# Sliding-window attention of a hybrid decoder layer: head pairs of one kv head, and a shared tile for both key blocks

## The chip, the cores and the metric

The kernel runs on one core of a Trainium2 chip. Five engines run their own instruction streams side by side and wait for each other through semaphores: TensorE (PE in the profile, its weight loads PEld), VectorE (DVE), ScalarE (ACT), GpSimd (POOL) and SyncE (SP), which here only issues DMAs. The metric is the device time of one execution in microseconds.

## The reference

One decoder layer of 1024 tokens and 1024 channels in float32; 16 learned meta tokens stand ahead of the sequence.

```python
z = rmsnorm(h, g_pre_mix) @ w_in              # q | k | v | x_rec | y_rec
# attention: 8 heads of 64, 2 kv heads (4 heads each), window of 128, one sink a head
valid = (diff >= 0) & (diff < WINDOW) & (kpos >= PAD)
s = where(valid, q k^T * 64**-0.5, NEG)
m = max(max(s), sink);  p = exp(s - m)
o = (p / (sum(p) + exp(sink - m))) @ v
# beside it: causal conv(4) -> gated linear recurrence on x_rec, times gelu(y_rec)
h = h + rmsnorm(concat(o, rec) @ w_out)
h = h + rmsnorm(relu(rmsnorm(h) @ w_ff1)**2 @ w_ff2)
```

Queries and keys are cut into blocks of 128. A query block sees its own key block (the triangle on and below the diagonal) and the one before it (the triangle above the diagonal); the two triangles together hold exactly 128 keys for each query. The block before the first holds only the 16 meta tokens.

## The kernel before

The matrix products are done in a fast float32 format of fewer bits. Operands are split into a high and a low part (`split`, L95 on ACT for the high and L98 on DVE for the low part; `split_scaled`, L116 and L117, the same out of an accumulator with a factor), and `mm3` adds three products (L124, L125, L126: high·high, high·low, low·high).

Stages: x and the meta tokens are loaded, normalised (L209, L215) and transposed. For each of four pieces of rows, `project` computes k, v, the first q and the first x. `put_k` (L355 to L357) takes K out of the accumulator: each kv head's 64 channels are written as high part on their own half of the partitions (ACT, L355), copied to the other half (DVE, L356), and the low part is written on the own half (DVE, L357). The other half of the low tile was set to zero.

Attention goes over four head pairs j and two halves of the sequence. A pair consists of head j and head j + 4, one of each kv head. `scores(j, half, q)` gives, for each head and four query blocks, matmuls of 256 keys (L518, L522), the minimum with mask and sink (L538, DVE), the exponential with its sum (L82, ACT), the reciprocal (L549) and the product with it (L551, DVE, one for each block). `attend(j, half, sn)` comes later: for each head it transposes 8 squares of 128 x 128 (L566, PE), splits them (L95, L98), and multiplies with V in pieces of 128, 256, 256, 256 and 128 queries, high and low each (L577). L591 (ACT) and L592 (DVE) add the two parts of the result. Between `scores` and `attend` of a pair stand other matmuls, taken from a list of fills: the projections q1, x1, q2, x2, x3, q3, y0 to y3. `conv` (L601, L606, DVE) follows each x.

After the attention, `gates(c)` multiplies x by block-diagonal gate weights (348 columns each). Their raw form is a tile of a slot of the kind "e", cleared by POOL (L675) and filled by four DMAs (L679). A sigmoid (L82) follows, then decay, recurrence (L720, L721), output projection and the feed-forward part.

All working tiles are taken from pools of a few kinds ("raw" 2 slots, "ws" 4, "a" 16, "b" 17, "c" 8, "d" 4, "e" 2); a new tile waits until the last user of its slot is done. PSUM has four kinds of two banks each (acc, s, pt, o). A scheduler orders each engine's instructions from priorities; `lut` keeps a written order on ACT's table functions.

Of the kernel before, what the change touches and what calls it, by code (L numbers as in the profile page):

```python
# [16 lines left out]
P = 128  # L17
# [20 lines left out]
def hybrid_layer(  # L38
# [23 lines left out]
    def pair(tag, shape):  # L62
        return slot(tag, shape, F32R), slot(tag, shape, F32R)
# [5 lines left out]
    def f32(ap):  # L69
        return ap.bitcast(F32)  # L70
# [118 lines left out]
        return hi, lo_  # L189

    def w_q(j):
        return load_cols(
            [((w_in, Q_COL + HD * j), HD), ((w_in, Q_COL + HD * (j + 4)), HD)]
        )

    def w_x_chunk(c):
        return load_cols([((w_in, X_COL + P * c), P)])
# [50 lines left out]
    khh = [slot("b", [P, T], F32R) for _ in range(2)]  # L248
    kl = [slot("b", [P, T], F32R) for _ in range(2)]
    HALF = (slice(0, HD), slice(HD, P))  # L250
    for h in range(2):
        nc.gpsimd.memset(f32(kl[h][HALF[1 - h]]), 0.0)

    zero = slot("ws", [P, 512])
    nc.vector.memset(zero, 0.0)
    km = const.tile([P, 4, P], F32R, name="km")
    vm = const.tile([P, 2, P], F32R, name="vm")
    nc.vector.tensor_copy(km.rearrange("p a b -> p (a b)"), zero)
    nc.vector.tensor_copy(vm.rearrange("p a b -> p (a b)"), zero[:, :256])

    flip = [0]

# [59 lines left out]
    xn = normed(0)  # L322
    rk = fetch([(K_COL, P)])
    rv = fetch([(V_COL, P)])
    rq = fetch([(Q_COL, HD), (Q_COL + 4 * HD, HD)], "e")
    load_x(2)
    load_x(3)
    rx = fetch([(X_COL, P)], "e")
# [22 lines left out]

    def put_k(hh, lo, src):
        for h in range(2):
            r, o = HALF[h], HALF[1 - h]
            nc.scalar.copy(hh[h][r], src[r])  # L355
            nc.vector.tensor_copy(hh[h][o], src[r])  # L356
            nc.vector.tensor_tensor(lo[h][r], src[r], f32(hh[h][r]), op=ALU.subtract)  # L357

    def sink_k(acc, t0, n):
        o = 0  # L360
        if t0 == 0:
            m = slice(0, NMETA)
            put_k(
                [km[:, 0, m], km[:, 1, m]], [km[:, 2, m], km[:, 3, m]], acc[:, m]
            )
# [6 lines left out]
    def sink_v(acc, t0, n):  # L372
        nc.scalar.copy(vt[:, t0 : t0 + n], acc)

    def new_q():
# [71 lines left out]
    nc.gpsimd.memset(mask1[:, 0:P], NEG)  # L447
    nc.gpsimd.memset(mask1[:, 0:NMETA], 0.0)
    nc.gpsimd.affine_select(
        out=mask1[:, 0:NMETA], in_=mask1[:, 0:NMETA], pattern=[[1, NMETA]],  # L450
        compare_op=ALU.is_gt, fill=NEG, base=P - NMETA, channel_multiplier=-1,
    )
    nc.gpsimd.tensor_copy(mask1[:, P:256], mask[:, P:256])


    lam = prm[:, :, 7]
# [26 lines left out]
            split(hi, lo, src[..., HALF[h]])  # L483

    pv = bank("o")
    nc.tensor.transpose(pv[:NMETA, :P], vt[:, :NMETA], ident)
    put_v([vm[:NMETA, 0, :], vm[:NMETA, 1, :]], pv[:NMETA, :P])
    for b in range(2):
        pv = bank("pt", (P, 4, P))
        for i in range(4):  # L490
# [10 lines left out]


    def scores(j, half, q):
        sn = [slot("c", [P, 4, 257]) for _ in range(2)]
        negm = small.tile([P, 2, 4], F32, name="negm", tag="negm")
        den = small.tile([P, 2, 4], F32, name="den", tag="den")
        rden = small.tile([P, 2, 4], F32, name="rden", tag="rden")
        for h in range(2):
            nc.vector.tensor_copy(
                sn[h][:, :, 256], nsink[:, j + 4 * h : j + 4 * h + 1].to_broadcast([P, 4])  # L510
            )
        for bp in range(2):
            for h in range(2):
                sp_ = bank("s", (P, 2, 256))

# [11 lines left out]
                for i in range(2):  # L527
                    b = 4 * half + 2 * bp + i
                    if b == 0:
                        qk(sp_[:, i, 0:P], b, km[:, h, :], km[:, 2 + h, :])  # L530
                        qk(sp_[:, i, P:256], b, khh[h][:, 0:P], kl[h][:, 0:P])
                    else:
                        c = slice((b - 1) * P, (b + 1) * P)
                        qk(sp_[:, i, :], b, khh[h][:, c], kl[h][:, c])
                for i in range(2):
                    b = 4 * half + 2 * bp + i
                    k = 2 * bp + i
                    nc.vector.tensor_tensor_reduce(  # L538
                        out=sn[h][:, k, 0:256], in0=sp_[:, i, :],
                        in1=mask1 if b == 0 else mask, scale=-1.0,  # L540
                        scalar=nsink[:, j + 4 * h : j + 4 * h + 1],
                        op0=ALU.add, op1=ALU.min, accum_out=negm[:, h, k : k + 1],
                    )
                    lut(
                        sn[h][:, k, :], sn[h][:, k, :], AF.Exp, scale=-1.0,
                        bias=negm[:, h, k : k + 1], accum_out=den[:, h, k : k + 1],
                    )
        for h in range(2):
            nc.vector.reciprocal(rden[:, h, :], den[:, h, :])  # L549
            for k in range(4):  # L550
                nc.vector.tensor_scalar(  # L551
                    sn[h][:, k, 0:256], sn[h][:, k, 0:256], rden[:, h, k : k + 1],
                    None, op0=ALU.mult,
                )
        return sn

    def attend(j, half, sn):
        flat = [t_.rearrange("p a b -> p (a b)") for t_ in sn]
        for h in range(2):
            ph, pl = pair("c", [P, 1024])  # L560
            for bp in range(2):
                pt = bank("pt")
                for i in range(2):
                    for s in range(2):
                        o = (2 * i + s) * P
                        nc.tensor.transpose(  # L566
                            pt[:, o : o + P],
                            sn[h][:, 2 * bp + i, s * P : (s + 1) * P], ident,
                        )
                c = slice(512 * bp, 512 * bp + 512)  # L570
                split(ph[:, c], pl[:, c], pt)
            po = bank("o")

            def av(kb, oc, n, pc, first, last):
                v = vm[:, h, :] if kb == 0 else vk[h][:, kb - 1, :]
                for k, p_ in enumerate((ph, pl)):
                    nc.tensor.matmul(  # L577
                        po[:, oc : oc + n], v, p_[:, pc : pc + n],
                        start=first and k == 0, stop=last and k == 1,
                        skip_group_check=True,  # L580
                    )

            kb0 = 4 * half
            av(kb0, 0, P, 0, True, False)
            for i in range(3):
                av(kb0 + 1 + i, i * P, 256, P + 256 * i, False, False)
            av(kb0 + 4, 3 * P, P, 7 * P, False, True)

            r, o = HALF[h], HALF[1 - h]
            part, whole = flat[h][r, 0:512], flat[0][r, 512:1024]  # L590
            nc.scalar.copy(part, po[o, :])  # L591
            nc.vector.tensor_tensor(whole, po[r, :], part, op=ALU.add)  # L592
# [139 lines left out]

    def load_wo(kc, tag):
        raw = slot(tag, [P, D])
        if kc < 4:
            nc.sync.dma_start(raw[0:HD, :], w_out[HD * kc : HD * kc + HD, :])
            o = HD * (kc + 4)
            nc.sync.dma_start(raw[HD:P, :], w_out[o : o + HD, :])
        else:
            nc.sync.dma_start(raw, w_out[P * kc : P * kc + P, :])  # L740
        wo_raw[kc] = raw

    wo = [None] * KC
# [600 lines left out]
```

## Time and profile before

| | |
|---|---|
| runs | 982.86, 986.53, 989.44 us (median 986.53) |
| profiled execution | span 984.1 us; no time is given for it apart from the span |
| PE | 955.5 us busy, 97%, 4782 matmuls |
| PEld | 803.2 us, 82% |
| DVE | 680.7 us, 69%, 1002 instructions |
| ACT | 502.3 us, 51%, 809 |
| POOL | 71.9 us, 7%, 108 |
| longest chain | PE 87%, DVE 5%, DMA 4%, ACT 2% |

The span runs from the first to the last recorded instruction. Busy time of PE counts modelled ends of pipelined matmuls, so neighbouring matmuls overlap. The chain is followed back from the last instruction, at each step to what released it. In the rows of groups, `out<-in` names the tiles, `x` the count, then busy time and mean nanoseconds of one, then the idle time ahead of it and who ended it. In the rows of the timeline the first number is the start, the second the length.

### The profile page before, as it was taken

What the parts mean: (1) busy time and instruction counts of PE and PEld (TensorE: products, weight loads), DVE (VectorE), ACT (ScalarE), POOL (GpSimd) and SP (SyncE); (2) the same over time, 40 slices, a digit from 0 to 9 for tenths busy, and PEclk for the clock granted to TensorE, in tenths of its full rate; (3) what the DMA queues carried; (4) which work ended last, traced back from release to release, by engine and by line L of the source; (5) the groups of instructions that cost most, each with busy time, mean ns of one, the idle gap of its engine ahead of it and who ended that gap; (6) DMA issues with size and microseconds to landing.
All of it is one profiled execution on the core that took longest, in us unless ns stands there. A gap on an engine that the chain in (4) does not pass through costs nothing.

```text
span 984.1 us, 12519 instructions
## 1 busy us (share of the span) xinstructions
PE 955.5 (97%) x4782; PEld 803.2 (82%) x4782; DVE 680.7 (69%) x1002; ACT 502.3 (51%) x809; POOL 71.9 (7%) x108
## 2 busy tenths in 40 slices
PE   6799999999999999999999999999999999999995
PEld 6798999889878887888888888888888788888874
DVE  6469997775885687665655465468567776779876
ACT  7356665457944554343555556654433343435331
POOL 4010000000002100000000000000111000002012
PEclk9799999999999999999999999999999999999998
DMA  8002100112134466576522364324678766647762
GB/s 282 23 12 63 25 23 22 43 44 65 65 129 147 149 216 193 173 256 200 197 96 86 97 202 130 106 88 122 167 182 190 182 224 190 193 152 191 226 182 85
DMA packets 89371, 133.28 MB, mean 135 GB/s; under 512 B 13752, under 2 KB 52680, under 8 KB 89312
## 3 DMA queue, kind: packets, MB, share of 16 engines
q1 hardware_dynamic: 81488, 112.04, 35.9%
q0 software_dynamic: 6960, 18.35, 8.8%
q10 hardware_dynamic: 864, 2.10, 0.6%
q8 instruction: 37, 0.61, 0.3%
q14 instruction: 22, 0.18, 0.1%
HBM read 113.60 MB, written 18.87 MB: 135 GB/s over the span
## 4 chain that ended last, share of the span: by engine, by line
PE 87%; DVE 5%; DMA 4%; ACT 2%; issue 1%; POOL 1%; POOLq 0%; SPq 0%; DVEq 0%; ACTq 0%
PE ps_acc L125 10%; PE ps_acc L124 10%; PE ps_acc L126 10%; PE ps_s L126 6%; PE ps_s L124 6%; PE ps_s L125 6%; PE ps_pt L124 6%; PE ps_pt L126 6%; PE ps_pt L125 6%; PE ps_o L125 5%; PE ps_o L124 5%; PE ps_o L126 5%; DMA raw<-in_w_ff_dram 2%; PE ps_o L577 2%; PE ps_pt L566 1%
## 5 line engine op out<-in xcount | busy, mean ns | idle before, releaser
L95 ACT CAST ws<-raw 128x1024 fp32r<-128x1024 f32 (+1 forms) x70 | 71.7, 1025 | 124.9 <-PE ps_o L125 47.7
L98 DVE TENSOR_TENSOR ws<-raw,ws 128x1024 fp32r<-128x1024 f32 (+1 forms) x71 | 84.7, 1194 | 54.7 <-ACT ws L95 54.5
L124 PE MATMUL ps_acc<-a,ws 128*128 128x256 f32 (+2 forms) x256 | 85.8, 335 | 0.1
L125 PE MATMUL ps_acc<-a,ws 128*128 128x256 f32 (+2 forms) x256 | 85.3, 333 | 0.0
L126 PE MATMUL ps_acc<-a,ws 128*128 128x256 f32 (+2 forms) x256 | 84.9, 332 | 0.0
L98 DVE TENSOR_TENSOR b<-b,b 128x1024 fp32r<-128x1024 f32 (+2 forms) x48 | 57.6, 1201 | 26.1 <-PE ps_o L125 18.6
L95 ACT CAST ws<-e 128x1024 fp32r<-128x1024 f32 x42 | 43.8, 1043 | 57.6 <-PE ps_o L125 27.6
L95 ACT CAST b<-b 128x1024 fp32r<-128x1024 f32 (+2 forms) x48 | 49.4, 1030 | 43.5 <-DVE b L860 41.5
L98 DVE TENSOR_TENSOR ws<-e,ws 128x1024 fp32r<-128x1024 f32 x42 | 51.4, 1223 | 21.4 <-ACT ws L95 21.4
L126 PEld LDWEIGHTS ps_acc<-a,ws 128*128 128x128 f32 x256 | 48.2, 188 | 4.4
L124 PEld LDWEIGHTS ps_acc<-a,ws 128*128 128x128 f32 x256 | 48.3, 189 | 4.2 <-ACT c L391 0.3
L125 PEld LDWEIGHTS ps_acc<-a,ws 128*128 128x128 f32 x256 | 48.2, 188 | 3.7
L125 PE MATMUL ps_acc<-ws,b 128*128 128x512 f32 (+1 forms) x120 | 46.5, 388 | 1.1 <-DVE ws L98 1.1
L124 PE MATMUL ps_acc<-ws,b 128*128 128x512 f32 (+1 forms) x120 | 46.3, 386 | 0.9 <-ACT ws L95 0.9
L169 POOL TENSOR_TENSOR rs<-ms,half_pow 128x1 f32<-128x1 f32 (+1 forms) x31 | 21.7, 704 | 347.3 <-DVE ms L165 345.9
L126 PE MATMUL ps_acc<-ws,b 128*128 128x512 f32 (+1 forms) x120 | 46.2, 385 | 0.0
L124 PE MATMUL ps_pt<-ws,b 128*128 128x512 f32 x112 | 44.2, 395 | 0.0
L126 PE MATMUL ps_pt<-ws,b 128*128 128x512 f32 x112 | 44.1, 394 | 0.0
L125 PE MATMUL ps_pt<-ws,b 128*128 128x512 f32 x112 | 44.1, 394 | 0.0
L124 PE MATMUL ps_s<-ws,b 128*128 128x512 f32 x110 | 43.4, 394 | 0.0
L125 PE MATMUL ps_s<-ws,b 128*128 128x512 f32 x110 | 43.3, 394 | 0.0
L126 PE MATMUL ps_s<-ws,b 128*128 128x512 f32 x110 | 43.2, 393 | 0.0
(382 smaller groups left out, 2688.6 us busy)
## 6 DMA issues: line engine op xcount, KB each, us to landing
raw<-in_w_ff_dram SPq DMA_DIRECT2D x66, 512.0 KB, 3.9
e<-in_w_ff_dram SPq DMA_DIRECT2D x47, 512.0 KB, 3.7
d<-in_w_ff_dram SPq DMA_DIRECT2D x12, 512.0 KB, 3.9
s_dram<-d POOLq DMA_DIRECT2D x12, 512.0 KB, 3.8
raw<-in_w_in_dram SPq DMA_DIRECT2D x9, 512.0 KB, 3.9
raw<-in_w_ff_dram POOLq DMA_DIRECT2D x9, 512.0 KB, 7.2
c<-in_x_dram SPq DMA_DIRECT2D x8, 512.0 KB, 8.1
d<-in_x_dram SPq DMA_DIRECT2D x8, 512.0 KB, 5.0
```

Source lines behind the costliest of these rows:

```text
L95: nc.scalar.copy(hi, src)
L98: low = nc.vector.tensor_tensor(lo, src, f32(hi), op=ALU.subtract).ins
L124: nc.tensor.matmul(dst, lh, rh, start=start, stop=False, skip_group_check=True)
L125: nc.tensor.matmul(dst, lh, rl, start=False, stop=False, skip_group_check=True)
L126: last_mm[0] = nc.tensor.matmul(dst, ll, rh, start=False, stop=stop, skip_group_check=True).ins.name
L169: last_pow[0] = nc.gpsimd.tensor_tensor(rs[:n], ms[:n], half_pow[:n], op=ALU.pow).ins.name
L566: nc.tensor.transpose(pt[:, o : o + P], sn[h][:, 2 * bp + i, s * P : (s + 1) * P], ident,)
L577: nc.tensor.matmul(po[:, oc : oc + n], v, p_[:, pc : pc + n], start=first and k == 0, stop=last and k == 1, skip_group_check=True,)
```

## The change

- Head pairs are now heads 2j and 2j + 1, both of kv head g = j // 2. The q weights come by one DMA of 128 columns instead of two of 64, the output weights too.
- K's high and low part are both mirrored to the other half of the partitions by SBUF-to-SBUF DMAs on SP's queue, after the second and the fourth piece; the copies on DVE and the zeros are gone.
- The meta tokens take the last 16 of 128 positions of the block before the first, and the rest of that block is zero, so that all blocks have one shape.
- Scores are handled in pairs of query blocks. POOL adds the exponentials of both key blocks into one 128 x 128 square for each head and block; DVE multiplies all four by the reciprocals at once. Four squares instead of eight are transposed, and split.
- GpSimd cuts each part (high, low) into the two triangles by `affine_select`.
- AV is one matmul of 512 (both heads, both blocks, both triangles where they share keys) and two of 256, high and low each.
- The result tile o_ of `attend` takes a slot of kind "e", and is written in pieces of 64 x 256.

```diff
     def put_k(hh, lo, src):
...
             nc.scalar.copy(hh[h][r], src[r])
-            nc.vector.tensor_copy(hh[h][o], src[r])
...
+    def mirror_k(c):
+        for h in range(2):
+            r, o = HALF[h], HALF[1 - h]
+            for t_ in (khh[h], kl[h]):
+                nc.sync.dma_start(f32(t_[o, c]), f32(t_[r, c]))
...
+        if b == 1:
+            for h in range(2):
+                r, o = HALF[h], HALF[1 - h]
+                nc.sync.dma_start(f32(km[o, h]), f32(km[r, h]))
+            mirror_k(slice(0, 512))
+        elif b == 3:
+            mirror_k(slice(512, T))
...
-        for h in range(2):
-            nc.vector.reciprocal(rden[:, h, :], den[:, h, :])
-            for k in range(4):
-                nc.vector.tensor_scalar(
-                    sn[h][:, k, 0:256], sn[h][:, k, 0:256], rden[:, h, k : k + 1],
-                    None, op0=ALU.mult,
-                )
+            nc.vector.reciprocal(rden, den)
+            one = sn[:, :, 0:P]
+            nc.gpsimd.tensor_tensor(one, one, sn[:, :, P:256], op=ALU.add)
+            nc.vector.tensor_tensor(one, one, rden.to_broadcast([P, 4, P]), op=ALU.mult)
+            pairs.append(sn)
...
+    def attend(j, half, pairs):
+        g = j // 2
+        o_ = slot("e", [P, 512])
+        for bp, sn in enumerate(pairs):
+            mh, ml = pair("c", [P, 4, 2, P])
+            pt = bank("pt", (P, 4, P))
             for k in range(4):
+                nc.tensor.transpose(pt[:, k, :], sn[:, k, 0:P], ident)
+            split(mh[:, :, 1, :], ml[:, :, 1, :], pt)
+            for m in (mh, ml):
+                for side, op, sign in ((0, ALU.is_gt, 1), (1, ALU.is_ge, -1)):
+                    nc.gpsimd.affine_select(
+                        out=m[:, :, side, :], in_=f32(m)[:, :, 1, :],
+                        pattern=[[0, 4], [-sign, P]], compare_op=op, fill=0.0,
+                        base=0, channel_multiplier=sign,
+                    )
+            po = bank("o", (P, 2, 256))
+            mhv, mlv = (m.rearrange("p (h i) s q -> p h (i s q)", h=2) for m in (mh, ml))
...
+            b = 4 * half + 2 * bp
+            av(vk[g][:, b, :], 0, 256, P, True, False)
+            av(vm[:, g, :] if b == 0 else vk[g][:, b - 1, :], 0, P, 0, False, False)
+            av(vk[g][:, b + 1, :], P, P, 3 * P, False, True)
+            c = slice(256 * bp, 256 * bp + 256)
+            for h in range(2):
+                r, o = HALF[h], HALF[1 - h]
+                nc.scalar.copy(o_[r, c], po[o, h, :])
+                nc.vector.tensor_tensor(o_[r, c], po[r, h, :], o_[r, c], op=ALU.add)
         ah, al = at[half][j // 2]
-        split(ah[:, j % 2, :], al[:, j % 2, :], flat[0][:, 512:1024])
+        split(ah[:, j % 2, :], al[:, j % 2, :], o_)
```

More of the change, by code (lines that the diff above doesn't have):

```diff
@@ L250, in hybrid_layer @@
     HALF = (slice(0, HD), slice(HD, P))
-    for h in range(2):
[L252 to L256, printed above, removed]
+    km = const.tile([P, 2, 2, P], F32R, name="km")
     vm = const.tile([P, 2, P], F32R, name="vm")
-    nc.vector.tensor_copy(km.rearrange("p a b -> p (a b)"), zero)
-    nc.vector.tensor_copy(vm.rearrange("p a b -> p (a b)"), zero[:, :256])
+    vmt = const.tile([P, P], F32, name="vmt")
+    nc.gpsimd.memset(f32(km), 0.0)
+    nc.gpsimd.memset(vmt, 0.0)
+    META = slice(P - NMETA, P)
     flip = [0]
@@ L446, in hybrid_layer @@
     mask1 = const.tile([P, 256], F32, name="mask1")
[L447 to L453, printed above, removed]
+    nc.gpsimd.memset(mask1[:, 0 : P - NMETA], NEG)
+    nc.gpsimd.tensor_copy(mask1[:, P - NMETA :], mask[:, P - NMETA :])
     lam = prm[:, :, 7]
@@ L485, in hybrid_layer @@
     pv = bank("o")
[L486 to L487 removed]
+    nc.tensor.transpose(pv[:, :P], vmt, ident)
+    put_v([vm[:, 0, :], vm[:, 1, :]], pv[:, :P])
     for b in range(2):
@@ L503, in scores @@
     def scores(j, half, q):
[L504 to L511, printed above, removed]
-        for bp in range(2):
+        g, pairs = j // 2, []
+        for bp in range(2):
+            sn = slot("c", [P, 4, 257])
+            negm = small.tile([P, 4], F32, name="negm", tag="negm")
+            den = small.tile([P, 4], F32, name="den", tag="den")
+            rden = small.tile([P, 4], F32, name="rden", tag="rden")
+            for h in range(2):
+                nc.vector.tensor_copy(
+                    sn[:, 2 * h : 2 * h + 2, 256],
+                    nsink[:, 2 * j + h : 2 * j + h + 1].to_broadcast([P, 2]),
+                )
             for h in range(2):
@@ L555, in scores @@
[L555 to L576, printed above, removed]
+                        scalar=nsink[:, 2 * j + h : 2 * j + h + 1],
@@ L581, in av @@
                     )
[L583 to L592, printed above, removed]
+            b = 4 * half + 2 * bp
[3 more added lines that the diff above has]
+            c = slice(256 * bp, 256 * bp + 256)
+            for h in range(2):
+                r, o = HALF[h], HALF[1 - h]
+                nc.scalar.copy(o_[r, c], po[o, h, :])
+                nc.vector.tensor_tensor(o_[r, c], po[r, h, :], o_[r, c], op=ALU.add)
         ah, al = at[half][j // 2]
-        split(ah[:, j % 2, :], al[:, j % 2, :], flat[0][:, 512:1024])
+        split(ah[:, j % 2, :], al[:, j % 2, :], o_)
     xc = [None] * NLRU
@@ L734, in load_wo @@
         raw = slot(tag, [P, D])
[L735 to L740, printed above, removed]
+        nc.sync.dma_start(raw, w_out[P * kc : P * kc + P, :])
         wo_raw[kc] = raw
```

38 lines of the change are left out of this document (20 added, 18 removed).

## The prediction

> **What bounds the kernel now.** I read the page's engine shares first, then windows of 50 us, since both programs issue the same TensorE instructions in the same order from the 1593rd of the changed one on (near 290 us); then the groups by form and the timelines.
>
> ```profile
> PE 955.5 (97%) x4782; PEld 803.2 (82%) x4782; DVE 680.7 (69%) x1002; ACT 502.3 (51%) x809; POOL 71.9 (7%) x108
> ...
> raw<-in_w_in_dram SPq DMA_DIRECT2D x9, 512.0 KB, 3.9
> ```
>
> ```profile
> 50.00:100.00 50.00, 49.88 (x379) 47.31 (x378) 40.28 (x122) 29.30 (x80) 2.71 (x4) 1.00 0.15 38
> 100.00:150.00 50.00, 50.00 (x386) 47.94 (x385) 46.95 (x142) 34.52 (x98) 0.00 (x0) 1.00 0.09 22
> 150.00:200.00 50.00, 49.50 (x316) 44.42 (x315) 37.60 (x76) 23.33 (x53) 0.00 (x0) 1.00 0.11 32
> ```
>
> The columns of a window are start and end, its length, busy time of PE, PEld, DVE, ACT and POOL, the granted clock, the DMA share and GB/s. In the stage of the attention PE is busy 149.4 of 150 us at full clock. A matmul taken away there comes off the time as long as nothing else makes PE wait. DVE stands second (46.95 of 50 in the densest window), DMA is at a tenth, and POOL does nothing at all from 100 us on. So the stage is bound by the number and spacing of PE's instructions, and the change moves work to the one engine that is empty.
>
> **PE's part.** A busy time overlaps with that of the next matmul, so the price is the distance of the starts.
>
> ```profile
> 107.63 0.63 PE L577 MATMUL ps_o<-c,b 128*128 128x128 f32 x4
> 108.09 0.38 PE L566 MATMUL ps_pt<-ident,c 128*128 128x128 f32 x2
> 108.23 0.77 PE L577 MATMUL ps_o<-c,b 128*128 128x256 f32 x5
> 108.84 0.84 PE L566 MATMUL ps_pt<-ident,c 128*128 128x128 f32 x6
> 109.44 0.36 PE L124 MATMUL ps_acc<-a,ws 128*128 128x256 f32 x1
> ```
>
> Four 128-wide AV matmuls take 108.09 − 107.63 = 0.46, 0.115 each; five 256-wide ones 0.61, 0.122 each; two and six transposes take 0.14 and 0.60, together 0.093 each. The 128-wide matmul costs nearly what the 256-wide one does. For the new 512-wide form I take the projections at the end of the stage:
>
> ```profile
> 203.03 0.40 PE L124 MATMUL ps_acc<-a,ws 128*128 128x512 f32 x1
> ...
> 208.32 0.40 PE L126 MATMUL ps_acc<-a,ws 128*128 128x512 f32 x1
> ```
>
> These are 23 steps in 5.29 us, 0.230 each. How many there are:
>
> ```profile
> L98 DVE TENSOR_TENSOR c<-ps_pt,c 128x512 fp32r<-128x512 f32 x32 | 21.7, 686 | 5.2 <-PE ps_o L577 2.8 <-ACT c L95 2.2
> ...
> L566 PE MATMUL ps_pt<-ident,c 128*128 128x128 f32 x128 | 19.3, 274 | 0.0
> L577 PE MATMUL ps_o<-c,b 128*128 128x256 f32 x96 | 18.4, 297 | 0.0
> ...
> L551 DVE TENSOR_SCALAR c<-c,rden 128x256 f32<-128x256 f32 x64 | 18.1, 350 | 0.3
> ...
> L592 DVE TENSOR_TENSOR c<-ps_o,c 64x512 f32<-64x512 f32 x16 | 10.9, 684 | 4.1 <-ACT c L591 3.9
> ...
> L577 PE MATMUL ps_o<-c,b 128*128 128x128 f32 x48 | 9.1, 247 | 0.5 <-DVE c L98 0.4
> ...
> L577 PE MATMUL ps_o<-c,vm 128*128 128x128 f32 x16 | 3.4, 232 | 0.0
> ```
>
> Half of the 128 transposes go: 64 × 0.10 (between 0.093 here and 0.115) = 6.4. The AV was 64 × 0.115 + 96 × 0.122 = 19.1; it becomes, per pair of query blocks and pair of heads (16 of them), two 512-wide and four 256-wide matmuls, 16 × (2 × 0.230 + 4 × 0.122) = 15.2. That is 3.9. Together 10.3; with the transposes at 0.115, 11.3. I take 10.7. (If the 512-wide AV, whose source is two pieces of 256, came at 0.25, that would be 32 × 0.02 = 0.6 less.) The score matmuls stay as many, as do the projections.
>
> The Trainium skill speaks against half of this: "TensorE: Matmul & The Clock Gate", section "Wait — 56ns, not 53.3ns?", gives 55.6 ns from start to start at N = 128 and 215.7 at N = 512, so that narrow matmuls cost by their width; by it the AV would save next to nothing and the transposes 64 × 0.0556 = 3.6, as an estimate −3.7 in place of −10.7. The rows above show 0.115 at full granted clock for the 128-wide, and I keep to the rows.
>
> **The start.** With K's high part mirrored by DMA, DVE loses its copies ahead of the low parts.
>
> ```profile
> 28.18 0.42 DVE L356 CAST b<-ps_acc 64x256 fp32r<-64x256 f32 x1
> ...
> 29.70 0.42 DVE L356 CAST b<-ps_acc 64x256 fp32r<-64x256 f32 x1
> 30.14 0.43 DVE L357 TENSOR_TENSOR b<-ps_acc,b 64x256 fp32r<-64x256 f32 x1
> ```
>
> ```profile
> 30.62 5.81 PE L237 MATMUL ps_acc<-a,ws 128*128 128x272 f32 x24 [5.56 <-DVE b L357]
> ```
>
> PE stands 5.56 us until the second low part is written at 30.57. The two copies of 0.42 ahead of it are gone, and two more of a few columns: −1.2 at most, −0.8 at least. I take −1.1. The ten mirror DMAs on SP's queue wait for K's sinks; behind those sinks PE still has its q and x projections of the same piece, 48 matmuls of 256, about 5.6 us at 0.117, and a DMA of a whole weight piece lands in 3.9 us (the row of the page above). I cost them at nothing; without that cover they cost 4 once. The weight pieces queued behind them on SP are for projections a whole head pair later.
>
> **The gates.** The output tile of an attend now takes a slot of the kind ("e", two of them) that holds the raw gate weights. Before, that slot was free at 52 us:
>
> ```profile
> 51.99 0.95 POOL L675 MEMSET e<- 128x1024 f32 x1
> 52.97 1.38 SPq L679 DMA_DIRECT2D e<-in_w_a_dram  x2
> ...
> 210.95 0.57 PE L124 MATMUL ps_s<-b,e 128*128 128x348 f32 x2
> 217.45 1.06 ACT L95 CAST b<-d 128x1040 fp32r<-128x1040 f32 x1
> ...
> 219.63 1.28 ACT L82 ACT_TABLE_LOAD   x1
> ```
>
> After, the clearing on POOL, four DMAs and the cast come behind the last attends: 0.95 + 1.4 of issue, 2 to land (half of the 3.9 of a piece of 512 KB) and 1.06 of a cast, about 5.4 us. The second half of y2 (24 × 0.230 = 5.5) just covers it. But the gates then stand without the last attends between them; ACT still has its casts (1.06 each) and the table load (1.28) before the first sigmoid, while PE has only six banks to fill. I reckon 1.28 + 1.06, about 2.4, as lost; at least 0, and at most 5 more if y2 does not cover the weights.
>
> **POOL's part** is the one that decides. For each of 16 block pairs it gets one addition of 128 × 512 and four triangle selections of 128 × 512. Rows near them:
>
> ```profile
> L1237 POOL TENSOR_TENSOR a<-a,a 128x512 f32<-128x512 f32 x3 | 4.0, 1334 | 12.7 <-ACT a L1183 12.7
> ```
>
> ```profile
> 3.44 0.30 POOL L437 MEMSET mask<- 128x256 f32 x1
> ...
> 4.37 0.29 POOL L438 TENSOR_SCALAR_AFFINE_SELECT mask<-mask 128x128 f32<-128x128 f32 x1
> 4.62 0.29 POOL L442 TENSOR_SCALAR_AFFINE_SELECT mask<-mask 128x128 f32<-128x128 f32 x1
> ```
>
> The addition is 1.33. The selection of 512 isn't in the trace; call its price p. If the memset's slope holds, (0.95 − 0.30) / 768 = 0.00085 per element, p = 0.29 + 384 × 0.00085 = 0.62; if everything scales, p = 4 × 0.29 = 1.16; by the distance of the two starts, 4 × 0.25 = 1.0. I take 0.75: memset and selection share their fixed part, 0.085 (0.30 − 256 × 0.00085); of the selection's 0.25 from start to start 0.165 then scale, times four 0.66, and with the fixed part 0.75. In all POOL gets 16 × (1.33 + 4 × 0.75) = 69 us, over the 150 us of the three windows: half, but not evenly. In the changed program's order, laid on the times of before, two stretches are dense: about 104 to 126 with 20 selections and 3 additions, and 137 to 154 with 16 and 2, where each AV stands on PE hardly behind its selections.
>
> The lock. POOL and DVE hold each other up:
>
> ```profile
> 27.40 0.75 DVE L215 TENSOR_SCALAR d<-c,rs 128x1024 f32<-128x1024 f32 x1
> ...
> 52.07 1.41 DVE L215 TENSOR_SCALAR d<-c,rs 128x1024 f32<-128x1024 f32 x1
> ```
>
> ```profile
> 968.51 1.07 DVE L165 SCALAR_TENSOR_TENSOR ms<-sq,late 128x1 f32<-128x1 f32 x1
> ...
> 970.11 0.14 DVE L165 SCALAR_TENSOR_TENSOR ms<-sq,late 128x1 f32<-128x1 f32 x1
> ```
>
> ```profile
> 968.28 1.29 POOL L1237 TENSOR_TENSOR a<-a,a 128x512 f32<-128x512 f32 x1 [12.70 <-ACT a L1183]
> ```
>
> The same operation on DVE takes 1.41 instead of 0.75 beside the memset at 51.99, and a step of 0.14 takes 1.07 until POOL's addition from 968.28 ends. So I count the DVE operations that read two tiles in the on-chip memory as POOL's time in the dense stretches. If all of DVE's work counted (the one at 52.07 reads a single tile), S below would be 0.94 × 39 + POOL's 33.7 − 39, about 31 us, but nothing shows that for the minima and products that make up most of it, so I stay with the two-input ones.
>
> The Trainium skill has a rule for it ("SBUF — State Buffer", "Who interferes with whom"): an exclusive lock of the shared ports, taken when DVE has two such inputs, or works in a two-port mode, and GpSimd reads there. By it the rows just quoted are waits for that lock, and the sum is mine below; the trace of before shows no selection beside a long two-input operation.
>
> ```profile
> 117.39 1.30 DVE L606 SCALAR_TENSOR_TENSOR d<-d,prm,d 128x1039 f32<-128x1039 f32 x1
> ```
>
> ```profile
> L98 DVE TENSOR_TENSOR ws<-raw,ws 128x1024 fp32r<-128x1024 f32 x14 | 17.1, 1223 | 10.1 <-ACT ws L95 10.1
> ...
> L98 DVE TENSOR_TENSOR b<-c,b 128x512 fp32r<-128x512 f32 x8 | 5.4, 686 | 0.7 <-ACT b L95 0.7
> ```
>
> First stretch: three such convolution steps of 1.30 and a first one of 0.8, a weight's low part 1.22, an output's 0.69, and three of the new products of 128 × 512 at 0.69: 8.7. POOL itself 20p + 4.0, in 22 us: 20p − 9.3 too much. Second stretch: 0.8 + 1.22 + 0.69 + 2 × 0.69 = 4.1, POOL 16p + 2.7, in 17 us: 16p − 10.2 too much. Both: S = 36p − 19.5, as PE has nothing else in its order that it could do first: 2.8 at p = 0.62, 7.5 at 0.75, 16.5 at 1.0, 22 at 1.16. What is late next is the score tiles behind it, so that it is not given back. The first two pairs and the last four have 2 to 4 us of other matmuls between selection and AV, and I cost them at nothing.
>
> **DVE and ACT** get lighter: for each of the eight pairs and halves DVE loses eight products (8 × 0.35), two low parts and two additions of 0.69 and gets two products of 0.69 and four additions of some 0.42: 5.6 less 3.1, about −2. They are not what PE waits for, so this counts for nothing but room for the lock.
>
> **Sum**, against the profiled execution's span of 984.1: −10.7 − 1.1 + 2.4 + 7.5 = −1.9, 982.2. The median of the runs shown lies 2.4 above the span: 984.6.
>
> **Rivals.** (1) POOL is hidden: p near 0.62 or the stretches less dense than I lay them, and the gates covered as before. For it: half of POOL's time is free even at 0.75. Against it: the memset and the lock rows. −10.7 − 1.1 = −11.8, 974.7 with the 2.4 between span and median.
>
> (2) Slower: POOL becomes the bound in the dense stretches, because the selection costs by its elements. One mechanism: AV waits for the second pair of selections. It turns the sum at 36p − 19.5 = 9.4, p = 0.80, and passes 1% at p = 1.08. For it: the only two rows of a selection stand at 0.25 to 0.29 for a quarter of the size; a selection beside a DVE operation can only be longer. Against it: the memset's slope. At p = 1.1, S = 20.1, +10.7, 997.2.
>
> (3) The gate weights come late, since POOL's clearing stands behind the last selections: up to 5 more than my 2.4. For it: y2's half covers by 0.5 only. Against it: POOL has 2 to 4 us to spare there. +3.1, 989.6.
>
> **How the numbers follow.** The forecast 0.50, with its own range of 979 (p = 0.62, and the gates' 2.4 partly hidden) to 991 (p = 0.92); rival 1 0.18, rival 2 0.24, rival 3 0.08. The range reaches to rival 1 at 975 and to p = 1.16 of rival 2, +12.6, about 1000. About 1% is what a measurement of this kernel can tell from no change: below 976.7 lies most of rival 1, 0.17; above 996.4 the upper part of rival 2 and what several stalls make together, 0.25; between them 0.58.
>
> **What would show it.** The mean of a selection on POOL (p) and the waits of AV on POOL; PE's idle time from 100 to 155 us, near 7 if I am right, none under rival 1, over 15 under rival 2. DVE's new products longer than 0.69 show the lock. PE's busy time down by some 10, 64 transposes at the old spacing, 512-wide AV at 0.230. The idle time before 36 us shorter by 1. An idle stretch of some 2 us at the gates, ended by ACT; ended by a DMA it is rival 3. Wrong altogether: PE waits for ACT or DVE in the attention, which I cost at nothing.

## The result, and the profile after

The changed kernel takes 981.11 us (median; 979.36 to 983.39), the kernel before 986.22 in the same comparison: a ratio of 0.9941, 95% interval 0.9917 to 0.9965. It is faster, by 0.6%, and inside the 1% that was called no change. The profiled execution's span is 979.4 us against 984.1, 4.7 less where 1.9 less was forecast.

The page's engine shares of the changed kernel, and its windows over the attention (the columns as in the prediction):

```profile
PE 946.1 (97%) x4654; PEld 790.9 (81%) x4654; DVE 666.8 (68%) x957; ACT 496.1 (51%) x810; POOL 142.5 (15%) x186
```

```profile
50.00:100.00 50.00, 49.03 (x365) 46.25 (x364) 38.75 (x117) 28.10 (x80) 17.52 (x18) 1.00 0.16 43
100.00:150.00 50.00, 47.12 (x336) 43.79 (x336) 44.74 (x124) 33.79 (x95) 31.65 (x36) 1.00 0.08 22
150.00:200.00 50.00, 47.91 (x283) 41.86 (x282) 35.96 (x77) 21.68 (x59) 18.15 (x21) 1.00 0.14 43
```

POOL's work went from nothing to 32 of 50 us in the dense window and DVE's fell by 2.2. PE's idle time in the three windows went from 0.1, 0 and 0.5 us to 1.0, 2.9 and 2.1. The groups by form that answer to the rows shown of before:

```profile
L576 POOL TENSOR_SCALAR_AFFINE_SELECT c<-c 128x512 fp32r<-128x512 f32 x64 | 49.7, 796 | 23.2 <-ACT c L95 8.8 <-DVE c L98 7.8 <-DMA raw<-in_w_in_dram 5.5
...
L560 POOL TENSOR_TENSOR c<-c 128x512 f32<-128x512 f32 x16 | 22.8, 1424 | 52.3 <-ACT c L82 52.2
...
L561 DVE TENSOR_TENSOR c<-c,rden 128x512 f32<-128x512 f32 x16 | 13.8, 861 | 5.3 <-POOL c L560 5.1
...
L586 PE MATMUL ps_o<-c,b 128*128 128x512 f32 x32 | 12.2, 402 | 1.6 <-POOL c L576 1.6
...
L572 PE MATMUL ps_pt<-ident,c 128*128 128x128 f32 x64 | 9.8, 273 | 0.0
...
L586 PE MATMUL ps_o<-c,b 128*128 128x256 f32 x56 | 9.2, 280 | 0.0
```

A selection takes 0.80 in the mean, but that is a mixture: 49 of the 64 take 0.63 to 0.67 and 15 take 0.99 to 1.64. The new product on DVE takes 0.86 instead of 0.69. PE's waits from 90 to 165 us, grouped (us in total, times, the longest):

```profile
PE ps_acc L124 <- ACT d L394: 2.2, 3, 0.9
PE ps_o L586 <- POOL c L576: 1.6, 2, 1.2
PE ps_s L526 <- ACT b L116: 1.5, 1, 1.5
PE ps_s L526 <- DVE rden L556: 0.5, 1, 0.5
```

That is 5.9 us of idle time, and only 1.6 of it names POOL directly. The rest names ACT and DVE, which were late in turn. The last two stalls show how, in PE's timeline, then POOL's, DVE's and ACT's. (A row of the timeline names the first form alone: the x6 are two matmuls of 512 columns and four of 256.)

```profile
156.37 1.08 PE L586 MATMUL ps_o<-c,b 128*128 128x512 f32 x6
158.67 1.17 PE L586 MATMUL ps_o<-c,b 128*128 128x512 f32 x6 [1.22 <-POOL c L576]
160.71 0.39 PE L124 MATMUL ps_acc<-a,ws 128*128 128x256 f32 x1 [0.87 <-ACT d L394]
```

```profile
150.76 7.81 POOL L576 TENSOR_SCALAR_AFFINE_SELECT c<-c 128x512 fp32r<-128x512 f32 x7
```

```profile
150.41 1.46 DVE L98 TENSOR_TENSOR ws<-raw,ws 128x1024 fp32r<-128x1024 f32 x1
151.80 1.13 DVE L609 TENSOR_SCALAR d<-d,prm 128x1040 f32<-128x1040 f32 x1
...
153.18 1.33 DVE L614 SCALAR_TENSOR_TENSOR d<-d,prm,d 128x1039 f32<-128x1039 f32 x1
...
155.59 0.82 DVE L517 COPY c<-nsink 128x2 f32<-128x2 f32 x4
...
156.79 1.28 DVE L614 SCALAR_TENSOR_TENSOR d<-d,prm,d 128x1038 f32<-128x1038 f32 x1
...
158.56 1.30 DVE L614 SCALAR_TENSOR_TENSOR d<-d,prm,d 128x1037 f32<-128x1037 f32 x1
```

```profile
159.88 0.37 ACT L599 COPY e<-ps_o 64x256 f32<-64x256 f32 x1 [2.02 <-PE ps_o L586]
160.27 0.66 ACT L394 COPY d<-ps_acc 128x272 f32<-128x272 f32 x2
```

Seven selections take 7.81 us, 1.12 each in the mean. Three of them take 0.63 to 0.67; the other four take 1.09 to 1.61 and lie beside a weight's low part (L98, itself 1.46 where its group in the prediction's rows had 1.22), the convolution's first step (L609, 1.13 where it took 0.80 at 116.39) and its taps (L614). AV waits for the selections. The last tap ends at 159.86, and before that ACT may not copy the next x out of PSUM (L394), since that x takes the slot which the convolution has read. In ACT's queue that copy also stands behind the copy of AV's result (L599), which became free within the same 0.02 us, so this place does not tell which of the two held it. PE has both banks full by then. Another place shows POOL and DVE holding each other up on both sides: an addition that takes 1.29 alone and a selection that takes 0.63, both drawn out around a tap that takes 1.30.

```profile
116.60 1.75 POOL L560 TENSOR_TENSOR c<-c 128x512 f32<-128x512 f32 x1
118.30 1.63 POOL L576 TENSOR_SCALAR_AFFINE_SELECT c<-c 128x512 fp32r<-128x512 f32 x1
```

```profile
117.77 1.68 DVE L614 SCALAR_TENSOR_TENSOR d<-d,prm,d 128x1039 f32<-128x1039 f32 x1
```

The same matmuls, laid side by side from the first to the last, show where the 4.7 us arose: −1.0 at 31 us, −2.2 at 39, −2.4 before the attention, −3.8 at 250 us, behind the attention and the gates, −3.0 at 320 us, −4.5 at the end. The last 1.5 lie in the feed-forward part, which is the same in both programs (the kernel before had two stalls there, 0.37 and 0.88, that the other didn't have); I do not count them as the change's.

### The profile page after: what moved, and what is told of

Its sections match the earlier page's. It is cut to its first block, busy times and chain, and to the rows that moved or that the text cites. A ratio compares the mean times of both kernels' runs of the same rounds, so it can differ in the third digit from the quotient of the medians.

```text
span 979.4 us, 12356 instructions
## 1 busy us (share of the span) xinstructions
PE 946.1 (97%) x4654; PEld 790.9 (81%) x4654; DVE 666.8 (68%) x957; ACT 496.1 (51%) x810; POOL 142.5 (15%) x186
## 4 chain that ended last, share of the span: by engine, by line
PE 78%; DVE 7%; ACT 6%; issue 3%; DMA 3%; POOL 3%; POOLq 0%; DVEq 0%; SPq 0%; ACTq 0%
PE ps_acc L125 8%; PE ps_acc L124 8%; PE ps_acc L126 8%; PE ps_pt L125 6%; PE ps_pt L126 6%; PE ps_pt L124 6%; PE ps_s L126 6%; PE ps_s L125 6%; PE ps_s L124 6%; PE ps_o L124 5%; PE ps_o L125 5%; PE ps_o L126 5%; ACT c L82 2%; DMA d<-in_w_ff_dram 1%; POOL c L576 1%
## 5 line engine op out<-in xcount | busy, mean ns | idle before, releaser
L98 DVE TENSOR_TENSOR ws<-raw,ws 128x1024 fp32r<-128x1024 f32 (+1 forms) x71 | 85.5, 1204 | 51.3 <-ACT ws L95 49.6
L98 DVE TENSOR_TENSOR b<-b,b 128x1024 fp32r<-128x1024 f32 (+2 forms) x48 | 57.6, 1200 | 26.3 <-PE ps_o L125 20.1
L98 DVE TENSOR_TENSOR ws<-e,ws 128x1024 fp32r<-128x1024 f32 x42 | 51.4, 1223 | 20.9 <-ACT ws L95 20.9
L576 POOL TENSOR_SCALAR_AFFINE_SELECT c<-c 128x512 fp32r<-128x512 f32 x64 | 49.7, 796 | 23.2 <-ACT c L95 8.8
L1124 POOL DMA_DIRECT2D raw<-in_w_ff_dram x9 | 10.9, 1208 | 266.1 <-DVE ws L98 200.2
L124 PE MATMUL ps_s<-ws,b 128*128 128x512 f32 x110 | 43.4, 395 | 0.0
```

The source lines that it names most:

```text
L98: low = nc.vector.tensor_tensor(lo, src, f32(hi), op=ALU.subtract).ins
L124: nc.tensor.matmul(dst, lh, rh, start=start, stop=False, skip_group_check=True)
L576: nc.gpsimd.affine_select(out=m[:, :, side, :], in_=f32(m)[:, :, 1, :], pattern=[[0, 4], [-sign, P]], compare_op=op, fill=0.0, base=0, cha ...
L1124: nc.gpsimd.dma_start(raws[0], w2v[q, a, b], accum_op=ADD)
```

## The experiments

All are edits of the changed kernel. Ratios are to the kernel before, on the same chip; spans are of one profiled execution, to be held against 979.4. "Idle time" is PE's. Against the changed kernel's own ratio of 0.9917 to 0.9965, four intervals lie apart: the selections doubled, the result tile in the score tile, AV in pieces (barely), and both left out. The others overlap with it, and what is said of them rests on the traces. The scheduler orders the instructions anew for every edit. Except for the run with the copy on DVE, each run has another order of PE's instructions in the attention, so that part of a small difference may be the order's.

**Half of the selections.**

```diff
-            for m in (mh, ml):
+            for m in (mh,):
                 for side, op, sign in ...
...
-                for k, m in enumerate((mhv, mlv)):
+                for k, m in enumerate((mhv, mhv)):
```

> The changed kernel without the two selections of the low part; AV reads the high part's triangles twice, so that the low part of the probabilities is left out. All matmuls, splits, additions and copies stay. POOL loses 32 selections of 0.63 to 1.1 each. Theory (GpSimd's selections, and the lock with DVE, cost the attention some 7 us through AV's waits and through what stands behind them on ACT): by S = 36p - 19.5 with half of the selections, S falls below zero; the idle time of PE from 90 to 165 us falls from 5.9 to under 1.5, span 5 to 7 shorter, 972.5 to 974.5. Rival (the stalls come from DVE and ACT queues in their own order, with conv and the sinks, and POOL only shares in them): at least half of the idle time stays, span 976 to 978.

Measured: span 975.6, ratio 0.9902 (0.9875 to 0.9930). The waits from 90 to 165 us:

```profile
PE ps_s L526 <- ACT b L116: 1.1, 1, 1.1
PE ps_acc L124 <- ACT d L394: 0.9, 1, 0.9
PE ps_acc L124 <- DVE b L117: 0.3, 1, 0.3
```

Idle time falls from 5.9 to 2.3: between the two expectations. 3.6 us hang on the low part: on its selections, and on AV's wait for DVE's low split (L98), which this edit takes away as well. No wait on POOL is left, and 2.3 stay that name ACT and DVE.

**Twice the selections.** Each is issued a second time.

```diff
-                    nc.gpsimd.affine_select(
+                    for _ in range(2):
+                        nc.gpsimd.affine_select(
...
```

> The changed kernel with each of the four selections of a block pair issued twice, with the same result: 64 more of them on POOL, at 0.63 each without and up to 1.1 with DVE beside it. Theory (the dense stretches pay each further microsecond of POOL in full, the others not): two stretches with 36 selections more, 36 x 0.65 to 0.8 = 23 to 29, span 1000 to 1008. Rival (POOL is mostly hidden, the 7 us are places where it meets conv): under 8 more, span below 988.

Measured: span 992.3, ratio 1.0078 (1.0054 to 1.0102). POOL's selections take 96.7 us instead of 49.7 (790 ns each, 128 of them). Idle time between 90 and 170 us grows to 11.5, by 5.5; one wait of AV is 5.2 long. The rest of the 12.9 goes with TensorE's clock, which in this execution fell to 0.50 to 0.88 in seven windows of 5 us at those stalls; (1 − clock) × 5 adds up to 8.6 us, some of which falls on idle time. Neither expectation was met: 64 more selections, 47 us of POOL, cost 12.9 in all and only 5.5 of it as waiting, where the rule asked for 23 to 29. My rule that each further selection in the dense stretches is paid in full is wrong.

**The addition on DVE.**

```diff
-            nc.gpsimd.tensor_tensor(one, one, sn[:, :, P:256], op=ALU.add)
+            nc.vector.tensor_tensor(one, one, sn[:, :, P:256], op=ALU.add)
```

> The changed kernel with the addition of the two key blocks' exponentials on DVE instead of POOL: 16 x 1.42 go from POOL, 16 x 0.69 = 11 come to DVE. Theory (POOL's queue and the lock decide, and an addition that waits for ACT's exponentials ahead of ready selections holds them up): PE's idle time in the attention falls from 5.9 to 2 to 4, span 2 to 4 shorter, 975.5 to 977.5. Rival (DVE is as full as POOL in the dense stretches, 45 of 48 us busy from 92 to 140): what POOL gives back DVE takes, span within 1 of 979.4 or up to 4 longer.

Measured: span 979.7, ratio 0.9978 (0.9960 to 0.9995). Idle time in the attention is 5.7, as before the edit; the clock took another 3.4. POOL lost 22.8 us and the mean selection became longer (847 ns): the rival. POOL's sum of work is not what binds; DVE's is as scarce.

**Without three of four taps.**

```diff
-        for k in (2, 1, 0):
+        for k in ():
```

> The changed kernel with three of the four taps of the convolution left out (the 12 DVE operations of 1.3 each that read two SBUF tiles); all else stays. Theory (what remains of the attention's loss is POOL's selections and DVE's taps holding each other up): the selections' mean falls from 0.80 to 0.63 to 0.70, PE's idle time between 90 and 165 us from 5.9 to under 2.0, no stretch at reduced clock there, span 974 to 976.5. Rival (the loss is the order of ACT's queue, where exponentials, sinks and the copies of AV's result wait behind each other, with or without taps): at least 4 of the 5.9 stay, span 977.5 to 980.

Measured: span 974.1, ratio 0.9893 (0.9851 to 0.9935). Idle time in the attention 0.65. The windows, then the selections' group:

```profile
90.00:140.00 50.00, 49.29 (x346) 45.32 (x345) 44.05 (x122) 35.41 (x100) 29.33 (x36) 1.00 0.12 33
140.00:165.00 25.00, 24.93 (x190) 23.72 (x190) 15.21 (x40) 11.82 (x31) 13.12 (x16) 1.00 0.08 23
```

```profile
L576 POOL TENSOR_SCALAR_AFFINE_SELECT c<-c 128x512 fp32r<-128x512 f32 x64 | 44.3, 710 | 28.4 <-ACT c L95 14.8 <-DMA raw<-in_w_in_dram 5.5 <-DVE c L98 5.4
```

All 64 selections are there and hardly anything waits for them. The rival falls, and the theory holds but for the selections' mean, 0.71 where at most 0.70 was expected: without the taps, six of which lie between 90 and 165 us, 5.3 of the 5.9 are gone. Nine drawn-out selections (0.97 to 1.61) are still there, most of them beside the new products, and cost PE hardly anything. What this run doesn't separate is the lock from DVE's plain load, since a tap is 1.3 us of DVE's queue also when POOL is idle. Which of the two makes the stalls stays open.

**Both left out.** The edits of the half selections and of the taps together.

> The changed kernel without three of four taps and without the low part's two selections (both parts of the computation left out, AV reads the high triangles twice): the attention with next to no lock and half of POOL's selections. It bounds what the stalls cost. Theory (the stalls of the attention come from POOL and DVE together, 5.9 of idle time and some 1.2 of restart): no idle time of PE over 0.2 from 90 to 165, span 979.4 - 5.9 - 1.2 = 972 to 973.5 at a clock of 0.994. Rival (ACT's order alone keeps 1 to 2.3 of it, as half selections did): 974 to 975.5.

Measured: span 971.2, ratio 0.9855 (0.9819 to 0.9890); no idle time from 90 to 165. The span is 8.2 us shorter. Laid side by side, 7.4 of that arise between 37 and 165 us, near the 5.9 of idle time and some 1.1 of restarts (below). The rest lies elsewhere: 0.3 at the gates and 1.0 near 940 us in the feed-forward part, less 0.5 at the start. So about 7 us is what these meetings of POOL and DVE cost.

**AV in pieces of 128.**

```diff
-                    nc.tensor.matmul(
-                        po[:, :, oc : oc + n], v, m[:, :, pc : pc + n],
+                    for h in range(2):
+                        for z in range(0, n, P):
+                            nc.tensor.matmul(
+                                po[:, h, oc + z : oc + z + P], v,
+                                m[:, h, pc + z : pc + z + P],
...
```

> The changed kernel with every AV matmul cut into pieces of 128 columns: 256 matmuls of 128 instead of 32 of 512 and 64 of 256, the same products, the same weights loaded for each piece. It measures the term by which the AV was predicted to save 3.9. By the rows of before (0.099 to 0.115 from start to start for a 128-wide AV matmul) the AV takes 25 to 29 instead of 14.9: 10 to 14 us more, some of it under the stalls that are there anyway: span 987 to 993. By the Trainium skill's figure of 55.6 ns it would take 14.2: span within 1.5 of 979.4.

The pieces of the first product each open the accumulation anew, so what is summed is not the same; number, width and waits are what is read here. Measured: span 984.5, ratio 0.9986 (0.9966 to 1.0006). From the timeline:

```profile
207.38 1.45 PE L588 MATMUL ps_o<-c,b 128*128 128x128 f32 x12
208.66 0.44 PE L126 MATMUL ps_acc<-a,ws 128*128 128x512 f32 x1
```

Twelve in 1.28 us: 0.107 each at full clock, not 0.056. The first of them stands 0.057 ahead of the second, the others 0.109 to 0.114 apart. 256 of them are 27.4, against 16 × 0.93 = 14.9 for the wide form. By that the span should grow by 12.5. It grew by 5.1, since all of the attention's idle time was gone (5.9, and some 1.1 of restarts): PE was slow enough for POOL. For a row of these matmuls, each with a weight load of its own, the trace differs by a factor of two from the 55.6 ns of the Trainium skill ("TensorE: Matmul & The Clock Gate", "Wait — 56ns, not 53.3ns?"), and the measurement decides; only the first of the twelve agrees with it. Whether it is the weight load that sets the distance, no run here separates.

**The result tile in the score tile.**

```diff
-        o_ = slot("e", [P, 512])
+        o_ = pairs[0].rearrange("p a b -> p (a b)")[:, 0:512]
```

> The changed kernel with the attention's result tile o_ put back into the (then free) score tile of its first block pair, instead of an "e" slot; nothing else is changed. The gate weights can then be loaded long before the gates. Theory (the gates lose about 1.4 us in the changed kernel because ACT and DVE cast weights and inputs together, behind the last attends): the weights' split moves out of that place, the idle time of PE at the gates falls from 0.2 + 0.8 to under 0.5, span 1 to 2 shorter than 979.4, so 977.5 to 978.5. Rival (the table load and the input casts alone set it, the weights are hidden): the same 0.8 to 1.1 of idle time and no change of the span within 1. A second rival: o_ in the score tile keeps that tile longer, the score tiles come late, and the attention loses 1 to 3.

Measured: span 985.8, ratio 1.0004 (0.9983 to 1.0026). The gates' idle time (0.2 + 0.8) is gone, as expected, and the time is longer. Behind the gates, and in the attention, the waits and the windows with a lower clock:

```profile
PE ps_pt L124 <- ACT b L95: 2.6, 1, 2.6
```

```profile
135.00:140.00 5.00, 3.34 (x20) 2.95 (x19) 4.91 (x17) 3.71 (x12) 0.60 (x1) 0.83 0.33 98
140.00:145.00 5.00, 5.00 (x38) 5.00 (x38) 4.40 (x14) 3.94 (x13) 2.16 (x3) 0.83 0.00 0
160.00:165.00 5.00, 2.84 (x11) 2.20 (x11) 3.19 (x8) 1.75 (x5) 3.44 (x5) 0.72 0.00 0
165.00:170.00 5.00, 5.00 (x29) 4.90 (x28) 0.23 (x2) 0.37 (x1) 0.00 (x0) 0.60 0.00 0
```

The wait for the recurrence's first operand grew from 1.1 to 2.6: what the gates gained was given back there, to ACT. The clock windows of the attention hold (0.17 + 0.17 + 0.28 + 0.40) × 5 = 5.1 us of lost clock, and 1.7 more lie behind the wait at the recurrence. In this order of the program, loading the gates' weights earlier gained nothing.

**The high part copied by DVE.**

```diff
             nc.scalar.copy(hh[h][r], src[r])
+            nc.vector.tensor_copy(hh[h][HALF[1 - h]], src[r])
...
-            for t_ in (khh[h], kl[h]):
+            for t_ in (kl[h],):
...
-                nc.sync.dma_start(f32(km[o, h]), f32(km[r, h]))
+                nc.sync.dma_start(f32(km[o, h, 1]), f32(km[r, h, 1]))
```

> The changed kernel with K's high part copied to the other half of the partitions by DVE out of the accumulator, as before, and only the low part mirrored by DMA. Theory (the start gains because the two copies of 0.42 no longer stand ahead of the low part that frees the accumulator): PE's idle time ahead of 30 us grows from 4.9 to 5.6 to 5.8, span 0.7 to 1 longer, and up to 2 more where the granted clock comes back later after the longer idle time: 980 to 982.5. Rival (the low part waits for ACT's high part or for other DVE work anyway): under 0.3 of idle time more, span within 0.5 of 979.4 at the same granted clock.

Measured: span 981.1, ratio 0.9972 (0.9942 to 1.0002). The idle time ahead of 30 us is 5.50 instead of 4.91, 0.6 more: just under the theory's 5.6 to 5.8, and not the rival's. The attention's waits are the same as in the changed kernel to within 0.05 us each; the clock was low for 1.7 us of them all the same.

**AV later in the order.**

```diff
+            with deferred(40):
                 b = 4 * half + 2 * bp
                 av(...)
...
                 nc.vector.tensor_tensor(o_[r, c], po[r, h, :], o_[r, c], op=ALU.add)
```

> The changed kernel with AV and what follows it in attend (the copy on ACT, the addition on DVE) given a later priority (by 40), so that in PE's order more projection matmuls stand between a block pair's transposes and its AV, by one or two groups of three in most places; POOL's selections get that time. Theory (AV comes before its selections are done, and what stands behind it on ACT is late in turn): PE's idle time between 90 and 165 us falls from 5.9 to 2 to 4, span 975.5 to 977.5. Rival (the copies and additions only come later too and meet the next scores on ACT and DVE; slots of kind c are held longer): the stall moves to the scores, span 979 to 982.

Measured: span 982.7, ratio 0.9972 (0.9952 to 0.9993). Idle time 5.7, with one wait of AV for POOL of 2.06 at 157.72. The rival, in the main: more room in PE's order only moved the stalls.

**Another slot for the fourth x.**

```diff
-            xr, sink = new_x()
+            xr, sink = new_x("b" if c == 3 else "d")
             project(w, ALL, sink)
-            conv(c, xr, "b" if c == 3 else "d")
+            conv(c, xr)
...
-            y = slot("b" if c == 1 else "d", [P, T])
+            y = slot("b" if c < 2 else "d", [P, T])
```

> The changed kernel, complete, with three slots exchanged: the input tile of the fourth x projection in a "b" slot instead of "d", its convolution's result in "d" instead of "b", the first y in "b" instead of "d". In the changed kernel the copy of that projection out of PSUM (ACT, two at once at 160.27) had to wait until the third convolution, held up beside seven selections, had read its own input from the same slot (its last tap ended at 159.86). Theory (a part of the loss is this handing on of a slot): the idle time of 0.87 ahead of 160.71 is gone, and the stall of AV ahead of it, 1.22 on POOL, stays or moves: span 0.5 to 1.5 shorter, 978 to 979 at a clock of 0.994; against before 0.992 to 0.994. Rival (ACT's copies of AV's result stand ahead of it anyway, and AV waits for POOL): the same idle time, span within 0.4.

Measured: median 979.19 (978.26 to 981.78), ratio 0.9920 (0.9892 to 0.9949). Both stalls at 158.67 and 160.71 are gone, 2.1 us; those up to 140 us are as they were. The waits from 90 to 165, and the clock behind the stall that stayed:

```profile
PE ps_s L526 <- ACT b L116: 1.5, 1, 1.5
PE ps_acc L124 <- ACT d L394: 1.4, 2, 0.9
PE ps_s L526 <- DVE rden L556: 0.6, 1, 0.6
PE ps_o L586 <- POOL c L576: 0.4, 1, 0.4
```

```profile
135.00:140.00 5.00, 2.52 (x13) 2.19 (x12) 4.84 (x17) 4.30 (x15) 1.91 (x2) 0.75 0.40 108
140.00:145.00 5.00, 5.00 (x27) 5.00 (x27) 2.17 (x8) 1.82 (x7) 0.64 (x1) 0.56 0.00 0
```

In the profiled execution (span 980.0) the clock took (0.25 + 0.44) × 5 = 3.5 us there, more than the stalls had been. It is faster than the kernel before; against the changed kernel the two intervals overlap, and only the trace shows that it waits less. That the slot alone did it is not shown: in this run's order 13 projection matmuls stand between the two AVs that followed each other directly, and PE came to the place later by the clock that it had lost.

## Why the prediction was right, point by point

The measured time lies in the range and within 1% of before, on the side of the forecast; the gain is 0.6% where 0.2% was forecast. Of the terms, PE's saving was somewhat too large, the start too small, the gates too large, and POOL's had the right size by a wrong rule. That their sum came out is in part luck.

- *PE saves 10.7.* Transposes and AV together take 30.8 us of start-to-start time before (added up over the timeline to 238 us) and 24.2 after, of which 3.1 are stalls among them: 9.7 saved. In it is a stall of some 0.6 that the kernel before had among its own, so the work itself fell by 9.1. The transposes fell by 6.6 (6.4 forecast), the AV by 3.2 with that stall (3.9 forecast). A block pair's AV takes 0.93, as 2 × 0.230 + 4 × 0.122 had it, but the old AV was taken too dear, 19.1 for 18.6. The rows that gave its price merge forms: the x4 at 107.63 are one matmul of 128 columns and three of 256, the x5 at 108.23 three of 256 and two of 128. In fact 41 of the 64 narrow ones stand only 0.056 to 0.063 ahead of the next matmul; where that next is one of 256 columns, the two together take 0.23, so that the narrow one still cost about half of it. For rows of narrow matmuls the forecast's 0.115 was near, as the run in pieces of 128 shows.
- *The start, −1.1.* The idle time shrank by 0.65 and the whole place by 0.9 up to 31 us. But 2.2 are there at 39 us: the term is mis-sized for want of the clock. The windows of before, then of after:

```profile
30.00:35.00 5.00, 4.38 (x19) 4.38 (x20) 1.78 (x8) 0.38 (x1) 0.00 (x0) 0.50 0.00 0
35.00:40.00 5.00, 5.00 (x38) 5.00 (x37) 0.12 (x1) 0.76 (x2) 0.00 (x0) 0.83 0.00 0
```

```profile
30.00:35.00 5.00, 5.00 (x33) 5.00 (x33) 1.09 (x10) 1.14 (x3) 0.00 (x0) 0.75 0.00 0
35.00:40.00 5.00, 5.00 (x45) 5.00 (x44) 1.33 (x3) 0.73 (x2) 0.00 (x0) 1.00 0.22 50
```

  Behind that idle stretch TensorE gets half of its clock for some us: before it lost 2.5 + 0.85 in these ten, after 1.25. That is an accident of the execution in part: with the same idle time of 4.9 the kernels of the experiments show 0.50 to 0.69 in the first of these windows. At 37 us the nine experiments with this start stand 0.2 to 1.5 us behind the changed kernel's trace, so the −2.2 is the lucky end of −0.7 to −2.2.
- *The gates, +2.4.* 0.2 + 0.8 of idle time, some 1.4 with the restarts, ended by ACT and DVE as said, not by a DMA (rival 3 falls). The recurrence's first operand costs 0.6 more than before (1.13 against 0.54 of idle time), which I had not counted.
- *POOL, +7.5.* Idle time of 5.9; counted from start to start, less the usual step, the seven stops cost 7.1. The price of a selection is 0.63 alone and 0.80 in the mean, on both sides of the 0.75 taken; the new products at 0.86 showed the lock. Right in size and place (90 to 161 us), but the rule S = 36p − 19.5 failed. It counts the lock apart, so p is the price alone, and 36 × 0.63 − 19.5 is 3.2; the 7.5 was near 7.1 only because p was guessed too dear, and that is luck. By the rule the doubled selections had to cost over 20, and cost 12.9, 5.5 of it waiting; half of them had to leave nothing, and left 2.3. The step that failed is "as PE has nothing else in its order that it could do first", by which all of POOL's excess in a dense stretch was to be paid. What took its place: the stalls arise at a few points where a convolution's taps and the selections come together, at most 2 us each. By the releasers that the waits name they reach PE mostly through DVE's and ACT's queues. Taking away the taps alone cleared 5.3 of 5.9, moving 23 us of POOL's work to DVE cleared nothing. Whether the lock itself or the taps' time in DVE's queue does it is not shown.
- *ACT and DVE counted for nothing.* Wrong: "PE waits for ACT or DVE in the attention" is where 4.3 of the 5.9 stand by name. Under "what would show it", this was the sign of being wrong altogether. The sum held because these waits, too, go when the taps and half of the selections go, so that the term put down to POOL's waits covered them.
- *Rival 2* (selections by their elements, over 0.80) did not come: 0.63 alone. *Rival 1* would have looked like the run without taps and half of the selections, at a span of 971.2.

The terms as measured, up to 320 us: −2.2 − 9.7 + 7.1 + 1.4 + 0.6 = −2.8, where the traces show −3.0. The stall that the kernel before had in its own attention is in the −9.7.

## What to carry to other kernels

Moving work to an idle engine need not be free: here GpSimd and VectorE held each other up, and the price showed at a few places where long operations of both came together, not as a sum over the stage. Follow a stall through the queues of the engines behind it, up to the slots that are handed on. And a saving on the bounding engine uncovers waits: by the starts the wide AV saved 12.5 us against the narrow one, and more than half of it went into waiting for the engines that feed it. When you price an instruction from a timeline, look whether the row merges several forms.

## What the runs showed of the hardware

- **The clock falls after short stops too.** In the attention of the kernel with the copy on DVE, two stops of 1.56 and 0.89 within some 3 us were followed by windows at 0.88 and 0.78; with the slot exchanged, the same two (1.54 and 0.94) by 0.75 and 0.56. In the changed kernel the same two were followed by full clock. So the loss is 0 to 3.5 us for the same two waits in three programs, and even stops of 1.35 and 0.30 were followed by a fall, in the run with the result tile in the score tile. What is lost comes in steps of 1.7 us: from 20 to 40 us it is 5.1 in the kernel before, 1.7 in the changed one, and 3.4 in seven of the ten experiments. The spans of a kernel go roughly with their mean clocks: the changed kernel has 977.8 at 0.995 and 981.7 at 0.991. The Trainium skill ("TensorE: Matmul & The Clock Gate", "Part 1: The HAM clock gate") says that the window in which activity is counted runs freely, so that it falls on a kernel differently from run to run, with which these traces agree; it puts the fall behind an idle window of about 3.4 us, and here 2.5 us of idle time in two parts, and once 1.65, were enough.
- **A selection of 128 × 512 on GpSimd** takes 0.63 alone, 1.08 where it met a product of 128 × 512 on VectorE, and 1.5 to 1.64 where it met a convolution tap or a weight's low part of 128 × 1024.
- **Each stop of TensorE costs some 0.16 us more than its idle time**, by the distance of the starts: seven stops, 5.9 idle, 7.1 lost.
